# Memory queries computed already turned, and POOL's query weights placed behind its normalising, in a two-layer encoder trunk

## The chip, the cores and the metric

The kernel runs on one core of a Trainium2 chip. The metric is the device time of one execution in microseconds. The kernel before has a median of 1107.18 us over three runs (1106.81 to 1107.87).

## The reference

The model is a trunk of two layers on 512 tokens of width 1024 (batch 1), with 12 token heads (three key/value heads, four query heads to each), 4 memory heads, head dimension 64, and 256 memory tokens. Cut to what matters:

```python
for i in range(2):
    h = rms_norm(x, g_mix_pre[i])
    proj = h @ w_in[i]                       # q 768 | k 192 | v 192 | qm 256 columns
    tok = mixer_a(q, k, v, sink)             # layer 0: window of +-128, partial rotary, sink
          # or mixer_b(q, k, v)              # layer 1: all keys, q/k norms, 2-D rotary
    mkv = rms_norm(mem, mem_norm_g) @ w_mem_kv[i]
    mo = memory_attention(qm, km, vm)        # softmax(qm km^T / 8) vm, no rotary, no norm
    x = x + rms_norm(concat([tok, mo]) @ w_o[i], g_mix_post[i])
    h = rms_norm(x, g_ffn_pre[i])
    x = x + rms_norm((silu(h @ w_gate) * (h @ w_up)) @ w_down[i], g_ffn_post[i])
```

All is fp32. The memory queries qm get no rotary turn and no norm; apart from the row's RMS factor and the scale 1/8 they are a plain product.

## The kernel before

**Products.** Every fp32 operand is split into a high part rounded to fp32r and a remainder in fp32r (`split`, L283: the high part by ACT at L289 or POOL at L287, the remainder by DVE at L293 or POOL at L291; `split_scaled`, L300, the same with a factor per row or column). A product is three matmuls, high x high, high x low, low x high (`mm3`, L277, lines 279 to 281). In the attention the two parts of a query stand one above the other on the 128 partitions, 64 and 64, and the keys are held twice, as (high, low) in `ka` and as (low, high) in `kb`, so that two matmuls give all four terms of a score. Weights come through `unit` (L215): a DMA on SP's queue into a raw tile, and then a split into a pair of tiles, in two parts (NPART). `PACE` says for each unit which engine splits it: 0 is ACT and DVE, 1 gives the remainder to POOL, 3 gives both to POOL. In layer 0 that is 3 for the units of the query groups 2 and 3. Layer 1's units of those groups were split earlier, in layer 0's feed-forward part, and are only fetched as pairs.

**Order of the work.** PE's order is written out by hand. `mixer` (L684) puts every piece of a layer's mixer into one list with a position x, counted in heads: head hg is scored at x = hg, turned and applied to the values 1.7 heads later. The list is sorted and run through. The other engines issue in an order that a scheduler draws up from the program's order and its own estimate of times; each engine then runs strictly in that order, and waits on semaphores.

**Queries.** Queries are made in four groups of four heads, c = 0 to 2 for the token heads and c = 3 for the memory heads (`q_pieces`, L517). For each of four tiles of 128 tokens, eight k-steps of three matmuls each (128 tokens x 256 columns) go into a bank of PSUM. ACT takes it out with the row factor (L541: for c = 3 that is `rq`, minus the RMS factor over 8), then for c < 3 a rotary turn by DVE follows (L443 to L446 in layer 0, with POOL in layer 1). ACT and DVE split it (`parts`), PE transposes the four heads, high and low part together, into a second bank (`stage`, L559), and ACT copies that to `qT` (L560). Group c has its products at about x = 4c - 5, so group 3 begins at x = 7.1 (layer 0) or 6.97 (layer 1) and takes four heads' time, a tile to each head; the positions 12 and later belong to the memory heads.

**Memory heads.** `mem_pieces` (L385) makes keys and values of the memory; `keys` (L422) turns them on PE (L427, L432), with copies by ACT (L429) to `ka` and by DVE (L433) to `kb`. The second turned product uses the single bank tagged pv. `score_mem` (L601) scores two query tiles at a time (L613, L614). As the queries carry a negative factor, DVE takes a minimum per row (L615), which is the bias of ACT's exponent, whose scale is the constant -1 (L618). `normalise` (L624) divides by the sum on POOL (L634); `turn` (L637) transposes the probabilities (L644) and splits them (L289, L293); `value` (L651) applies them (L658, L659) and puts the head's two halves together by ACT (L666) and DVE (L667).

**Banks.** PSUM's eight banks go by tags: acc has two, s three in rotation, t two, pv one. The attention-out product (`heads_out`, L804) begins at x = 11.4 (11.3), before the memory heads, and takes acc, acc and s for its first three tiles.

**Start.** Layer 0's key/value products of the first two tiles (`kv_pieces`, L470, product lines L489 and L490) run in the order of the table `FIRST`: (tile, pair of k, kind), where HH is high x high, LH the low part of x, HL the low part of the weights. The parts of x are made by ACT (L306), POOL (L304) and DVE (L307).

Of the kernel before, what the change touches and what calls it, by code (L numbers as in the profile page):

```python
# [9 lines left out]
F32 = mybir.dt.float32  # L10
# [6 lines left out]
P = 128  # L17
S = 512
# [16 lines left out]
URGENT = 150  # L35
HH, HL, LH = range(3)
FIRST = ((0, 0, HH), (0, 1, HH), (0, 0, LH), (0, 1, LH), (0, 0, HL), (0, 1, HL), (1, 0, HH), (1, 1, HH), (1, 0, HL), (1, 1, HL),
         (0, 2, HH), (1, 2, HH), (0, 2, LH), (0, 3, HH), (1, 3, HH), (0, 3, LH), (1, 0, LH), (1, 1, LH), (1, 2, LH),
# [150 lines left out]
class Trunk:  # L189
    def __init__(self, tc, a):  # L190
        self.tc, self.nc, self.a, self.nraw, self.more, self.early = tc, tc.nc, a, 0, None, {}
        self.pairs, self.todo, self.stores = {}, [], []

# [20 lines left out]

    def unit(self, src, side=0, pool=None, parts=1, put=None, x=0, dst=None, key=None, g=None, raw=None, pair=None, early=None):  # L215

# [39 lines left out]
        box = []  # L256

        def first():
            box.append(load())
            dst[key] = box[0][1:]  # L260
            part(box[0], 0, n // NPART)

        put(x, first)
        for z in range(1, NPART):
            put(x + z / 4, lambda z=z: part(box[0], z * n // NPART, (z + 1) * n // NPART))

# [155 lines left out]
    def keys(self, k2, ka, kb, t, n):  # L422

        nc = self.nc
        tp = self.ps.tile([P, 4, P], F32, tag="t", name="tp", bufs=2)
        for h in range(n):
            nc.tensor.transpose(tp[:, h].bitcast(F32R), k2[:, h, :P], self.identr)  # L427
        c = slice(t * P, (t + 1) * P)
        nc.scalar.activation(ka[:, :, c], tp[:, :n], AF.Copy)  # L429
        tp = self.tagged("pv", "tp").rearrange("p (h n) -> p h n", n=P)  # L430
        for h in range(n):
            nc.tensor.transpose(tp[:, h].bitcast(F32R), k2[:, h, HD:], self.identr)  # L432
        nc.vector.tensor_copy(kb[:, :, c], tp[:, :n])  # L433

# [35 lines left out]
    def kv_pieces(self, l):  # L470
# [6 lines left out]
        def prod(t, st, u, which=None):  # L477
            self.ready(t)
            if u == 0 and which in (None, HH):
                st["ps"] = self.tagged("acc" if t < 2 else "s")  # L480
            ps = st["ps"]
            for k in (2 * u, 2 * u + 1):
# [3 lines left out]
                if which is None:  # L486
                    self.mm3(*args, k == 0, k == KD - 1)
                else:
                    nc.tensor.matmul(args[0], args[1 + (which == LH)], args[3 + (which == HL)],  # L489
                                     start=which == HH and k == 0, stop=which == HL and k == KD - 1)  # L490
            if u == 3 and which in (None, HL):
# [25 lines left out]
    def q_pieces(self, l, c, qTs, put, x0, lead):  # L517
        nc = self.nc
        w = {}
        for z in range(2):  # L520
            self.unit(self.a["wq"][l, c, z], self.side(l, "qw", 2 * c + z), put=put, x=x0 - lead + z * lead / 3, dst=w,
                      key=z, pair=("wq", l, c, z), early=("wq", z) if l == c == 0 else None)

        def prod(t, st, u):
# [10 lines left out]
            if u == 3:  # L535
                qx = self.core.tile([P, 4, HD], F32, tag="qx", name="qx", bufs=3)
                q = ps[:, :256].rearrange("p (h d) -> p h d", d=HD)
                if l == 1 and c < 3:
                    nc.scalar.activation(qx, q, AF.Copy, scale=self.rs[:, t:t + 1])
                else:  # L540
                    nc.scalar.activation(qx, q, AF.Copy, scale=self.rq[:, t:t + 1])  # L541
                st["qx"], st["r"] = qx, None
                if c < 3:
                    st["r"] = self.rope(l, qx, t, 4, 0)

# [7 lines left out]
        def stage(t, st):  # L553
            if c:
                tp = self.tagged("s" if c == 3 and t > 1 else "acc", "tp").rearrange("p (h n) -> p h n", n=P)
            else:
# [10 lines left out]
        return out  # L567


    def score(self, hd, i):  # L570
# [30 lines left out]
    def score_mem(self, hd, i):  # L601
# [9 lines left out]
        for z in range(2):  # L611
            qi = hd["q"]()[:, (i + z) * P:(i + z + 1) * P]
            nc.tensor.matmul(s[:, z], qi, hd["ka"](), start=True, stop=False)  # L613
            nc.tensor.matmul(s[:, z], qi, hd["kb"](), start=False, stop=True)  # L614
        nc.vector.tensor_reduce(nm[:, i:i + 2], s, axis=AX.X, op=OP.min)  # L615
        for z in range(2):
            p = self.core.tile([P, self.pbufs[0]], F32, tag="p", name="p", bufs=self.pbufs[1])
            nc.scalar.activation(p[:, :NMEM], s[:, z], AF.Exp, bias=nm[:, i + z:i + z + 1], scale=-1.0,  # L618
                                 accum_out=den[:, i + z:i + z + 1])
            hd["p"].append(p)  # L620
# [3 lines left out]
    def normalise(self, hd):  # L624
# [7 lines left out]
        for z, (k0, k1) in enumerate(hd["rng"]):  # L632
            n = (k1 - k0) * P
            self.pooled = nc.gpsimd.tensor_scalar(hd["p"][z][:, :n], hd["p"][z][:, :n], rd[:, z:z + 1], 1.0,  # L634
                                                  op0=OP.mult, op1=OP.mult)

# [47 lines left out]
    def mixer(self, l, mkp, late, tokp):  # L684
# [70 lines left out]
        self.mem_pieces(l, mk, put, xm, [pc["m0dur"], pc["m0dur"], pc["mdur"], pc["mdur"]], pc["mlag"], xw)  # L755
        for c in range(1, 4):
            x0 = 4 * c - 5 + pc["qoff"][c - 1]
            lay(self.q_pieces(l, c, qT, put, x0, pc["qlead"]), x0, pc["qstep"], pc["qlag"], lambda t, c=c: 4 * c + (t / 4 if c < 3 else t // 2 / 2 * pc["hstep"]))
        heads()
# [612 lines left out]
```

## Time and profile before

| | |
|---|---|
| profiled execution | 1108.23 us, of which the span of instructions is 1106.4 |
| median of three runs | 1107.18 us |
| granted TensorE clock | 0.998 |
| layer 0's mixer | from the start to about 166 us |
| layer 1's mixer | about 545 to 726 us |
| TensorE waited most for (all in the mixers) | DVE tl L293 2.6 us, DVE tok L667 2.4 us, DVE wlo L293 1.3 us |

The profile is of one execution, by the hardware's own recording. PE is TensorE's matmul, PEld its weight load, DVE VectorE, ACT ScalarE, POOL GpSimd, SP the queue of DMAs. A row of the timeline gives start, duration, engine, line of the kernel, operation, what it writes and reads, and in brackets how long the engine stood idle before and what ended that. Matmuls overlap: the time that one takes from the engine is the distance to the next one's start, not its duration.

### The profile page before, as it was taken

Reading aid. Unit: us, or ns where it says so; the run is one execution under the profiler, and the core shown is the slowest. Engines: PE = TensorE matmul, PEld = TensorE weight load, DVE = VectorE, ACT = ScalarE, POOL = GpSimd, SP = SyncE. Lnnn points to the kernel's source line nnn. Section 1 sums busy time; section 2 is a strip of 40 time slices with the busy share of each in tenths; the row PEclk is TensorE's granted clock in tenths of the full one; section 3 lists DMA queues with packets and bytes.
Section 4 is the critical chain, followed back from the end, with each engine's and each line's share of the span. In section 5 each row is a group of like instructions: output and inputs, shape, how many; then the busy total and the mean of one; then the engine's idle time right before and its main releaser. Section 6 shows DMA issues by size and latency. Waiting matters only on the chain.

```text
span 1106.4 us, 19515 instructions
## 1 busy us (share of the span) xinstructions
PE 1088.8 (98%) x7436; PEld 1000.2 (90%) x7436; DVE 842.2 (76%) x1433; ACT 659.3 (60%) x1357; POOL 194.9 (18%) x341
## 2 busy tenths in 40 slices
PE   9999999999999999999999999999999999999997
PEld 7899888999889989998898888879998899899986
DVE  7889876999458677875888988758995478668854
ACT  7679975865435535553567888747664365346531
POOL 5773231102000000000444542312000000000001
PEclk9999999999999999999999999999999999999999
DMA  9621017354832562335533221154236133422253
GB/s 335 248 78 39 20 35 252 116 165 133 303 124 86 180 221 78 113 101 190 195 124 115 77 77 39 39 189 154 72 106 207 55 100 115 129 76 97 83 165 115
DMA packets 40702, 142.44 MB, mean 129 GB/s; under 512 B 4768, under 2 KB 5152, under 8 KB 40480
## 3 DMA queue, kind: packets, MB, share of 16 engines
q1 hardware_dynamic: 40320, 140.80, 37.7%
q8 instruction: 58, 0.95, 0.4%
q10 hardware_dynamic: 288, 0.40, 0.1%
q14 instruction: 36, 0.29, 0.1%
HBM read 122.30 MB, written 18.87 MB: 128 GB/s over the span
## 4 chain that ended last, share of the span: by engine, by line
PE 84%; DVE 6%; ACT 4%; POOL 2%; DMA 2%; issue 1%; DVEq 0%; SPq 0%; POOLq 0%; ACTq 0%
PE ps L280 13%; PE ps L279 13%; PE ps L281 13%; PE ps L1043 12%; PE ps L1042 12%; PE ps L1041 12%; PE tp L644 3%; PE o L659 2%; PE o L658 2%; PE s L583 1%; PE s L584 1%; DVE mT L307 1%; ACT whi L289 1%; DVE tl L293 1%; DMA row<-in_x_dram 1%
## 5 line engine op out<-in xcount | busy, mean ns | idle before, releaser
L289 ACT ACTIVATE whi<-raw 128x1024 fp32r<-128x1024 f32 (+3 forms) x206 | 169.2, 839 | 175.9 <-PE ps L1043 73.5
L293 DVE TENSOR_TENSOR wlo<-raw,whi 128x1024 fp32r<-128x1024 f32 (+3 forms) x202 | 191.2, 961 | 74.5 <-ACT whi L289 71.3
L1042 PE MATMUL ps<-sf,wlo 128*128 128x256 f32 x640 | 179.7, 281 | 0.0
L1041 PE MATMUL ps<-sf,whi 128*128 128x256 f32 x640 | 179.7, 281 | 0.0
L1043 PE MATMUL ps<-sf,whi 128*128 128x256 f32 x640 | 179.7, 281 | 0.0
L280 PE MATMUL ps<-wlo,f 128*128 128x512 f32 (+1 forms) x360 | 138.6, 385 | 0.1
L279 PE MATMUL ps<-whi,f 128*128 128x512 f32 (+1 forms) x360 | 138.7, 385 | 0.0
L281 PE MATMUL ps<-whi,f 128*128 128x512 f32 (+1 forms) x360 | 138.4, 384 | 0.0
L1043 PE MATMUL ps<-a,whi 128*128 128x256 f32 x480 | 134.4, 280 | 0.0
L1041 PE MATMUL ps<-a,whi 128*128 128x256 f32 x480 | 134.3, 280 | 0.0
L1042 PE MATMUL ps<-a,wlo 128*128 128x256 f32 x480 | 133.8, 279 | 0.0
L1042 PEld LDWEIGHTS ps<-sf,wlo 128*128 128x128 f32 x640 | 121.4, 190 | 0.5
L1041 PEld LDWEIGHTS ps<-sf,whi 128*128 128x128 f32 x640 | 121.1, 189 | 0.5
L1043 PEld LDWEIGHTS ps<-sf,whi 128*128 128x128 f32 x640 | 121.4, 190 | 0.0
L322 POOL TENSOR_SCALAR e<-sso 128x1 f32<-128x1 f32 x8 | 3.4, 423 | 564.1 <-ACT junk L317 564.0
L634 POOL TENSOR_SCALAR p<-p,rd 128x256 f32<-128x256 f32 (+2 forms) x128 | 76.7, 618 | 101.4 <-DVE rd L631 46.2
L279 PE MATMUL ps<-whi,hT 128*128 128x256 f32 (+1 forms) x304 | 92.6, 305 | 0.0
L1042 PEld LDWEIGHTS ps<-a,wlo 128*128 128x128 f32 x480 | 90.5, 188 | 0.2
L1041 PEld LDWEIGHTS ps<-a,whi 128*128 128x128 f32 x480 | 90.4, 188 | 0.2
L1043 PEld LDWEIGHTS ps<-a,whi 128*128 128x128 f32 x480 | 90.1, 188 | 0.0
L280 PE MATMUL ps<-wlo,hT 128*128 128x256 f32 (+1 forms) x304 | 88.5, 291 | 1.3 <-DVE wlo L293 1.3
L281 PE MATMUL ps<-whi,hT 128*128 128x256 f32 (+1 forms) x304 | 88.2, 290 | 0.0
(207 smaller groups left out, 2703.9 us busy)
## 6 DMA issues: line engine op xcount, KB each, us to landing
raw<-in_wgu_dram SPq DMA_DIRECT2D x48, 512.0 KB, 4.5
raw<-in_wd_dram SPq DMA_DIRECT2D x44, 512.0 KB, 4.4
rb<-in_wgu_dram SPq DMA_DIRECT2D x40, 512.0 KB, 3.6
raw<-in_wo_dram SPq DMA_DIRECT2D x17, 512.0 KB, 4.1
raw<-in_wq_dram SPq DMA_DIRECT2D x16, 512.0 KB, 5.0
xt<-x SPq DMA_DIRECT2D x12, 512.0 KB, 5.2
raw<-in_wm_dram SPq DMA_DIRECT2D x8, 512.0 KB, 4.5
x<-y SPq DMA_DIRECT2D x8, 512.0 KB, 3.1
```

The lines of the kernel that those rows point to most:

```text
L279: mm(out, lh, rh, start=first, stop=False)
L280: mm(out, lh, rl, start=False, stop=False)
L281: mm(out, ll, rh, start=False, stop=last)
L289: a = nc.scalar.activation(hi, src, AF.Copy)
L293: b = nc.vector.tensor_sub(lo, src, hi.bitcast(F32))
L634: self.pooled = nc.gpsimd.tensor_scalar(hd["p"][z][:, :n], hd["p"][z][:, :n], rd[:, z:z + 1], 1.0, op0=OP.mult, op1=OP.mult)
L644: nc.tensor.transpose(tp[:, z], hd["p"][i][:, jj * P:(jj + 1) * P], self.ident)
L658: nc.tensor.matmul(o[:, c0:c1], hd["v"](j), th, start=(j == 0), stop=False, skip_group_check=True)
L659: nc.tensor.matmul(o[:, c0:c1], hd["v"](j), tl, start=False, stop=last, skip_group_check=True)
L1041: mm(out, wh[:, s], rh, start=start and k == 0, stop=False, skip_group_check=True)
L1042: mm(out, wl[:, s], rh, start=False, stop=False, skip_group_check=True)
L1043: mm(out, wh[:, s], rl, start=False, stop=k == 3, skip_group_check=True)
```

## The change

Five things are done at once.

1. The memory queries leave `q_pieces` and get a function of their own. The weights become the stationary operand, 128 columns (two heads) at a time, and 512 tokens stream past: two products z = 0, 1 of eight k-steps, each into an acc bank that holds two heads' queries with the head dimension on the partitions. No transposes follow. ACT copies head h of a bank to its own 64 partitions of `qT` as high part (`high`), DVE writes the remainder to the other 64 (`low`): for the odd heads the high part stands below, which the two forms of the keys allow. The eight k-steps of z = 0 take the two heads' time from x = 7.1, those of z = 1 the next two; the copies come at 0 and 0.5 (0 and 0.25) of a head after the end of the product, the remainders 0.2 (0.15) later.
2. These queries carry no factor. So `score_mem` takes a maximum, DVE multiplies it by `rq` (128x2), and the exponent's scale is a column of `rp` = -`rq`, made once per layer by POOL.
3. The copy of the memory keys to `kb` goes to ACT (token keys stay with DVE).
4. In layer 0 POOL's splits of query weights are issued behind the normalising of a certain head: group 2's units behind heads 0 and 1, group 3's behind heads 3 and 4.
5. In `FIRST`, tile 0's HH and LH of the first two pairs of k become H2: for each k, HH and then LH, where all HH ran first, then all LH.

```diff
-HH, HL, LH = range(3)
-FIRST = ((0, 0, HH), (0, 1, HH), (0, 0, LH), (0, 1, LH), (0, 0, HL), (0, 1, HL), (1, 0, HH), ...
+BEHIND = {(0, 2, 0): 0, (0, 2, 1): 1, (0, 3, 0): 3, (0, 3, 1): 4}
+HH, HL, LH, H2 = range(4)
+FIRST = ((0, 0, H2), (0, 1, H2), (0, 0, HL), (0, 1, HL), (1, 0, HH), ...
...
 def unit(...):
+        def behind(c0, c1):
+            with nullcontext() if after is None else self.tc.issue_after(self.pooled[after].ins):
+                part(box[0], c0, c1)
...
 def keys(...):
-        nc.vector.tensor_copy(kb[:, :, c], tp[:, :n])
+        if n == NMH:
+            nc.scalar.activation(kb[:, :, c], tp[:, :n], AF.Copy)
+        else:
+            nc.vector.tensor_copy(kb[:, :, c], tp[:, :n])
...
+    def memory_queries(self, l, qTs, put, x0, lead, step):
+        nc = self.nc
+        w, ps = {}, {}
+        for z in range(2):
+            self.unit(self.a["wq"][l, 3, z], self.side(l, "qw", 6 + z), put=put, x=x0 - lead + z * lead / 3, dst=w,
+                      key=z, pair=("wq", l, 3, z), after=BEHIND.get((l, 3, z)))
+        def prod(z, k):
+            if k == 0:
+                ps[z] = self.tagged("acc")
+            c = slice((k % 4) * 256 + P * z, (k % 4) * 256 + P * z + P)
+            wh, wl = [x[:, c] for x in w[k // 4]]
+            self.mm3(ps[z], wh, wl, self.hslice(0, k, 0, S), self.hslice(1, k, 0, S), k == 0, k == KD - 1)
+        rows = (slice(0, HD), slice(HD, P))
+        def high(z, h):
+            if z == h == 0:
+                qTs[3] = self.core.tile([P, 4, S], F32R, tag="qT", name="qT", bufs=2)
+                self.rp = self.small.tile([P, NT], F32, tag="rp", name="rp", bufs=2)
+                nc.gpsimd.tensor_scalar(self.rp, self.rq, -1.0, 1.0, op0=OP.mult, op1=OP.mult)
+            nc.scalar.activation(qTs[3][rows[h], 2 * z + h], ps[z][rows[h]], AF.Copy)
+        def low(z, h):
+            q = qTs[3][:, 2 * z + h]
+            nc.vector.tensor_sub(q[rows[1 - h]], ps[z][rows[h]], q[rows[h]].bitcast(F32))
+        for z in range(2):
+            for k in range(KD):
+                put(x0 + (2 * z + k / 4) * step, lambda z=z, k=k: prod(z, k))
+            for h in range(2):
+                x = x0 + 2 * (z + 1) * step + h * (0.25 if z else 0.5)
+                put(x, lambda z=z, h=h: high(z, h))
+                put(x + (0.15 if z else 0.2), lambda z=z, h=h: low(z, h))
...
 def score_mem(...):
-        nc.vector.tensor_reduce(nm[:, i:i + 2], s, axis=AX.X, op=OP.min)
+        mx = self.small.tile([P, 2], F32, tag="mx", name="mx", bufs=3)
+        nc.vector.tensor_reduce(mx, s, axis=AX.X, op=OP.max)
+        nc.vector.tensor_mul(nm[:, i:i + 2], mx, self.rq[:, i:i + 2])
...
-            nc.scalar.activation(p[:, :NMEM], s[:, z], AF.Exp, bias=nm[:, i + z:i + z + 1], scale=-1.0,
+            nc.scalar.activation(p[:, :NMEM], s[:, z], AF.Exp, bias=nm[:, i + z:i + z + 1],
+                                 scale=self.rp[:, i + z:i + z + 1],
                                  accum_out=den[:, i + z:i + z + 1])
...
 def mixer(...):
-        for c in range(1, 4):
+        for c in range(1, 3):
...
+        self.memory_queries(l, qT, put, 7 + pc["qoff"][2], pc["qlead"], pc["qstep"])
```

`issue_after` ties only the order on the named instruction's engine, here POOL.

More of the change, by code (lines that the diff above doesn't have):

```diff
@@ L213, in ahead, with unit @@
             self.stores = [(self.pairs[(name, *at)][z], pair[z].bitcast(F32)) for z in range(2)]
-    def unit(self, src, side=0, pool=None, parts=1, put=None, x=0, dst=None, key=None, g=None, raw=None, pair=None, early=None):
+    def unit(self, src, side=0, pool=None, parts=1, put=None, x=0, dst=None, key=None, g=None, raw=None, pair=None, early=None, after=None):
         nc, n = self.nc, src.shape[-1]
@@ L260, in first @@
             dst[key] = box[0][1:]
-            part(box[0], 0, n // NPART)
+            behind(0, n // NPART)
         put(x, first)
         for z in range(1, NPART):
-            put(x + z / 4, lambda z=z: part(box[0], z * n // NPART, (z + 1) * n // NPART))
+            put(x + z / 4, lambda z=z: behind(z * n // NPART, (z + 1) * n // NPART))
     def raw(self):
@@ L478, in prod @@
             self.ready(t)
-            if u == 0 and which in (None, HH):
+            if u == 0 and which in (None, HH, H2):
                 st["ps"] = self.tagged("acc" if t < 2 else "s")
@@ L488, in prod @@
                 else:
-                    nc.tensor.matmul(args[0], args[1 + (which == LH)], args[3 + (which == HL)],
-                                     start=which == HH and k == 0, stop=which == HL and k == KD - 1)
+                    for z in (HH, LH) if which == H2 else (which,):
+                        nc.tensor.matmul(args[0], args[1 + (z == LH)], args[3 + (z == HL)], start=z == HH and k == 0,
+                                         stop=z == HL and k == KD - 1)
             if u == 3 and which in (None, HL):
@@ L521, in q_pieces @@
             self.unit(self.a["wq"][l, c, z], self.side(l, "qw", 2 * c + z), put=put, x=x0 - lead + z * lead / 3, dst=w,
-                      key=z, pair=("wq", l, c, z), early=("wq", z) if l == c == 0 else None)
+                      key=z, pair=("wq", l, c, z), early=("wq", z) if l == c == 0 else None, after=BEHIND.get((l, c, z)))
         def prod(t, st, u):
@@ L537, in prod @@
                 q = ps[:, :256].rearrange("p (h d) -> p h d", d=HD)
-                if l == 1 and c < 3:
+                if l:
                     nc.scalar.activation(qx, q, AF.Copy, scale=self.rs[:, t:t + 1])
@@ L554, in stage @@
             if c:
-                tp = self.tagged("s" if c == 3 and t > 1 else "acc", "tp").rearrange("p (h n) -> p h n", n=P)
+                tp = self.tagged("acc", "tp").rearrange("p (h n) -> p h n", n=P)
             else:
@@ L755, in mixer @@
         self.mem_pieces(l, mk, put, xm, [pc["m0dur"], pc["m0dur"], pc["mdur"], pc["mdur"]], pc["mlag"], xw)
-        for c in range(1, 4):
+        for c in range(1, 3):
             x0 = 4 * c - 5 + pc["qoff"][c - 1]
-            lay(self.q_pieces(l, c, qT, put, x0, pc["qlead"]), x0, pc["qstep"], pc["qlag"], lambda t, c=c: 4 * c + (t / 4 if c < 3 else t // 2 / 2 * pc["hstep"]))
+            lay(self.q_pieces(l, c, qT, put, x0, pc["qlead"]), x0, pc["qstep"], pc["qlag"], lambda t, c=c: 4 * c + t / 4)
+        self.memory_queries(l, qT, put, 7 + pc["qoff"][2], pc["qlead"], pc["qstep"])
         heads()
```

12 lines of the change are left out of this document (5 added, 7 removed).

## The prediction

> **What bounds the kernel now.** I read the page first, then the idle time of TensorE (the view of waits), then busy times by stretch, then the timeline of the stretches that the change touches.
>
> ```profile
> PE 1088.8 (98%) x7436; PEld 1000.2 (90%) x7436; DVE 842.2 (76%) x1433; ACT 659.3 (60%) x1357; POOL 194.9 (18%) x341
> PE 84%; DVE 6%; ACT 4%; POOL 2%; DMA 2%; issue 1%; DVEq 0%; SPq 0%; POOLq 0%; ACTq 0%
> ```
>
> TensorE is busy 98% of the span and holds 84% of the chain that ended last. So a matmul that is no longer issued is worth its slot, unless another engine ends last where it stood. The stretches with busy times (us: length, PE, PEld, DVE, ACT, POOL) show two such places beside this change:
>
> ```profile
> 120.00:138.00 18.00, 16.58 (x122) 15.29 (x121) 16.77 (x47) 17.73 (x52) 4.62 (x9) 1.00 0.10 30
> 680.00:690.00 10.00, 9.35 (x57) 7.78 (x56) 9.23 (x17) 9.95 (x24) 2.70 (x4) 1.00 0.19 76
> ```
>
> In the last part of layer 0's token heads ACT is busy 17.73 of 18 us and PE 16.58; in layer 1's, ACT 9.95 of 10 and PE 9.35. There a saved matmul can turn into idle time.
>
> **The transposes that go.** The turned product gives queries with head dimensions on the partitions, so the memory queries' 16 transposes per layer (four groups of four, L559) are removed. PE's timeline around one group:
>
> ```profile
> 676.32 0.60 PE L644 MATMUL tp<-cst,p 128*128 128x128 f32 x4
> 676.67 0.54 PE L559 MATMUL tp<-identr,q 128*128 128x128 f32 x4
> 677.05 0.35 PE L279 MATMUL ps<-whi,hT 128*128 128x256 f32 x1
> ```
>
> The group holds PE from 676.67 to the next start at 677.05: 0.38 us (its 0.54 us overlaps the next). Two layers times four groups: 8 x 0.38 = 3.0 us.
>
> **The products.** Per layer 4 tiles x 8 k x 3 = 96 matmuls of 256 columns become 2 x 8 x 3 = 48 of 512. Starts three matmuls apart:
>
> ```profile
> 679.21 0.28 PE L279 MATMUL ps<-whi,hT 128*128 128x256 f32 x1
> ...
> 679.57 0.28 PE L279 MATMUL ps<-whi,hT 128*128 128x256 f32 x1
> ...
> 689.36 0.40 PE L279 MATMUL ps<-whi,th 128*128 128x512 f32 x1
> ...
> 690.06 0.39 PE L583 MATMUL s<-ka,qT 128*128 128x512 f32 x1
> ```
> ```profile
> 399.82 0.39 PE L279 MATMUL ps<-whi,f 128*128 128x512 f32 x1
> ...
> 400.50 0.39 PE L279 MATMUL ps<-whi,f 128*128 128x512 f32 x1
> ```
>
> 256 columns take 0.36/3 = 0.120 us, 512 columns 0.70/3 = 0.233 here in the mixer and 0.68/3 = 0.227 in the down product. 96 x 0.120 = 11.5 against 48 x 0.233 = 11.2 or 48 x 0.227 = 10.9: 0.3 to 0.6 us per layer. The rows are rounded, so I take near the low end, 0.35, and 0.7 us for both. PE's work falls by 3.7 us.
>
> **ACT and DVE.** Median durations (min/median/max ns) of what goes and of the nearest rows to what comes:
>
> ```profile
> L541 ACT ACTIVATE qx<-ps,rq x20: 453/466/502, 28.9 to 682.5; 128x256 f32<-128x256 f32 x20
> L289 ACT ACTIVATE q<-qx x32: 400/417/438, 33.6 to 687.1; 128x256 fp32r<-128x256 f32 x32
> L560 ACT ACTIVATE qT<-tp x32: 575/598/629, 48.5 to 695.2; 128x512 fp32r<-128x512 f32 x32
> L666 ACT ACTIVATE tmp<-o x32: 589/594/597, 71.5 to 724.6; 64x512 f32<-64x512 f32 x32
> L618 ACT ACTIVATE p<-s,nm x32: 462/472/506, 136.5 to 716.9; 128x256 f32<-128x256 f32 x32
> L293 DVE TENSOR_TENSOR q<-qx,q x32: 407/426/805, 41.4 to 687.6; 128x256 fp32r<-128x256 f32 x32
> L667 DVE TENSOR_TENSOR tok<-o,tmp x32: 672/688/697, 72.1 to 725.2; 64x512 f32<-64x512 f32 x32
> L631 DVE RECIPROCAL rd<-den x32: 160/174/180, 61.7 to 717.5; 128x4 f32<-128x4 f32 x32
> ```
>
> Per layer ACT loses 4 x (0.47 + 0.42 + 0.60) = 5.9 us and gains four copies of 64x512 (4 x 0.59 = 2.4, by L666; half the partitions cost what the whole does) and two key copies of 128x512 (0.6 each, by L560). DVE loses four q remainders (1.7) and the two key copies, and gains four remainders of 64x512 (4 x 0.69 = 2.8, by L667) and eight products of 128x2 (at most 8 x 0.17 = 1.4, by the reciprocal).
>
> In 120 to 138 ACT loses about half of the 5.9 us and gains the second half's two copies, so near 2 us net; DVE there trades two q remainders for two larger ones, about even. DVE's 16.77 us then ends last where ACT's 17.73 did: the stretch may shrink by some 0.7 us while PE would shrink by about 1.2 (two to three groups and half the products' gain). I put 0.5 us as given back (bounds: 0.8 gained, 1.2 given back). In layer 1 the idle time is one wait:
>
> ```profile
> 686.36 0.30 PE L644 MATMUL tp<-cst,p 128*128 128x128 f32 x1 [0.65 <-DVE tl L293]
> ```
>
> It hangs on ACT's queue, not on PE; PE comes some 1.5 us earlier (three groups and the products), ACT about half a us to none. I put 0.5 us given back (bounds: 0.4 gained, 1.0 given back).
>
> The exponent now takes its scale from a column of 128x1 instead of a constant. L541 has such a scale and costs 0.466 for 256 columns where L289, without, costs 0.417, so 0 to 0.1 us each, 16 per layer; with the product behind the maximum, the chain score, maximum, exponent grows by 0.2 to 0.3 us. The memory heads' stretch has room on all three but for the end, where TensorE waits for the previous head's output:
>
> ```profile
> 722.83 0.47 PE L658 MATMUL o<-th,vm 128*128 128x512 f32 x1 [0.68 <-DVE tok L667]
> ```
>
> That wait is DVE's queue; I put +0.25 us for both layers (0 to 1.0). The Trainium skill (ScalarE: Activation LUTs, section What ACT_TABLE_LOAD costs) says each 128x1 pointer operand adds about 93 ns to an ACTIVATE. Those rows lie between none and that; by the page ACT gets back 32 x 0.093 = 3.0 us of its relief, an estimate, and the sum stays, since this stands where ACT has room.
>
> **The memory keys' copy.** The second turned product of a key tile (L432) uses the one bank tagged pv, so the next tile's must wait until the first is copied out. That copy moves from DVE to ACT, behind ACT's queue. Layer 1, PE, ACT, and PE again where the first head is turned; then layer 0:
>
> ```profile
> 598.92 0.50 PE L432 MATMUL tp<-identr,k 128*128 128x128 f32 x4
> ```
> ```profile
> 599.15 0.60 ACT L429 ACTIVATE kma<-tp 128x512 fp32r<-128x512 f32 x1
> 599.63 0.71 ACT L595 ACTIVATE p<-s,nm 128x512 f32<-128x512 f32 x1
> ```
> ```profile
> 603.21 0.38 PE L644 MATMUL tp<-cst,p 128*128 128x128 f32 x2
> 603.80 0.33 PE L644 MATMUL tp<-cst,p 128*128 128x128 f32 x1 [0.22 <-POOL p L634]
> ```
> ```profile
> 60.30 0.50 PE L432 MATMUL tp<-identr,k 128*128 128x128 f32 x4 [0.77 <-DVE kmb L433]
> ```
>
> In layer 1 the second tile's product starts at 598.92 unhindered. ACT starts the first tile's other copy only at 599.15; the moved copy can follow at 599.7 and ends near 600.4: PE, and all behind it in order, waits 1.5 us. About 0.9 us of it comes back at 603, where PE idles for head 0's probabilities in two steps (the last of three matmuls that should need 0.1 us each starts 0.6 late, and another wait follows). Net +0.55 (0 to 1.5). In layer 0 the wait of 0.77 for DVE becomes one for ACT: +0.15 (-0.8 to +0.3).
>
> **POOL and the first products.** POOL's timeline in layer 0:
>
> ```profile
> 74.28 1.30 POOL L291 TENSOR_TENSOR wlo<-raw,whi 128x512 fp32r<-128x512 f32 x1
> 75.56 2.25 POOL L634 TENSOR_SCALAR p<-p,rd 128x256 f32<-128x256 f32 x4
> ...
> 88.34 2.10 POOL L634 TENSOR_SCALAR p<-p,rd 128x256 f32<-128x256 f32 x4 [4.52 <-ACT th L289]
> ```
>
> Head 2's normalising stood behind weight splits; the memory weights now come behind heads 3 and 4, where POOL idles 4.52 us before head 4: room for one unit's two remainders (1.30 each) and its two roundings. The weights are needed only at 7.1 heads by the program's order, two heads on. I put -0.3 (-0.6 to +0.6).
>
> At the start, xh wh and xl wh now alternate:
>
> ```profile
> 6.61 2.40 PE L489 MATMUL ps<-whi,hT 128*128 128x384 f32 x8 [0.20 <-ACT whi L289]
> ...
> 9.54 1.10 PE L489 MATMUL ps<-whi,hT 128*128 128x384 f32 x4
> ```
> ```profile
> 8.98 1.54 POOL L304 TENSOR_SCALAR hT<-xT,gcol 128x128 fp32r<-128x128 f32 x4
> ```
>
> The eight take 2.40 us; back to back they would take about 1.6 (seven starts 0.174 apart, an estimate midway between the slots of 256 and 512 columns, and a last one of at most 0.4): 0.8 us of gaps while ACT makes the next weights, which the xl products can fill; so the 9.54 group could start 0.5 us earlier. But that group needs tile 1's odd columns from POOL, whose run from 8.98 ends at 10.52: it stays. I take 0 (0.5 gained at best).
>
> **Sum.** -3.7 + 0.5 + 0.5 + 0.25 + 0.55 + 0.15 - 0.3 + 0 = -2.05 us. The profiled execution took 1108.23 us for a span of 1106.4, 1.05 above the median 1107.18, so its sum would be 1106.2; put on the median, 1105.1 us.
>
> **Rivals.** *All of the removed work lands*: the waits at the keys and in the two ACT-bound stretches don't come, because ACT's lighter queue runs ahead of where the rows show it. For: 5.9 us per layer off ACT where it is fullest. Against: DVE is nearly as full. -3.7 - 0.3 = -4.0: 1103.2 us.
>
> *POOL's splits hold up DVE.* A DVE product of 128x64 took 1.29 us while POOL split weights, 0.29 while it did not:
>
> ```profile
> 55.25 1.29 DVE L443 TENSOR_TENSOR rt<-qx,cst 128x64 f32<-128x64 f32 x1
> ...
> 60.48 0.29 DVE L443 TENSOR_TENSOR rt<-qx,cst 128x64 f32<-128x64 f32 x1
> ```
> ```profile
> 53.91 2.56 POOL L291 TENSOR_TENSOR wlo<-raw,whi 128x512 fp32r<-128x512 f32 x2
> ```
>
> The splits move on behind heads 0, 1, 3 and 4, the last two near 84 to 95 us, beside the rotary products; some 1.5 us of DVE delay there reach PE: 1106.6 us. The Trainium skill (SBUF — State Buffer, section Who interferes with whom) has the rule: DVE with two SBUF inputs and a reading GpSimd exclude each other for a whole instruction. The trace agrees in this place (1.29 against 0.29).
>
> *The second bank comes free late: slower.* Each half of the queries keeps one acc bank until its last remainder is off; the attention-out product's second tile (L279, 689.36 above) needs the second half's bank. Today the last tile leaves its bank early and its remainder follows late:
>
> ```profile
> 682.47 0.50 ACT L541 ACTIVATE qx<-ps,rq 128x256 f32<-128x256 f32 x1
> ...
> 687.57 0.61 DVE L293 TENSOR_TENSOR q<-qx,q 128x256 fp32r<-128x256 f32 x1 [0.16 <-ACT q L289]
> ```
>
> If that lag of 5.1 us stays, the last remainder, placed a quarter of a head later (heads 2 and 4 on POOL are 12.8 us apart, so 1.6 us) and behind another of 0.69, runs from 689.9 to 690.5, while PE wants the bank at 689.36 - 1.5 = 687.9: a wait of 2.6 us per layer. -2.05 + 5.3 = +3.2: 1110.4 us. It decides from a lag of about 2.5 us on. Against: two steps instead of four, straight from the bank, and ACT relieved.
>
> **Chances.** The forecast 0.50 (1104.0 to 1106.6 us), all lands 0.26, POOL 0.12, the bank 0.12. A measurement of this kernel tells about 0.2%, 2.2 us, from no change, so faster means below 1105.0: the second case and two fifths of the first, 0.46; slower 0.12; the same 0.42. The range runs from 1102.4, a little below the full gain, to 1108.0, where the bank's case begins: 0.18 left out.
>
> **What would show it.** No L559 in the last quarter of the token heads, 48 products of 128x512 at 0.23; L432's wait on ACT near 600; DVE instead of ACT as the fullest engine in 120 to 138; first group at 9 us, then a longer wait for POOL; the attention-out product's waits. It is wrong if the mixers' idle time on PE changes by over 3 us, whatever the sum.

## The result and the profile after

The changed kernel takes 1113.82 us (median of 4 runs, 1113.30 to 1114.34) where the kernel before, run beside it, takes 1106.99 (1106.72 to 1107.87, 4 runs): a ratio of 1.0057 [1.0045, 1.0069], so 6.8 us slower. The prediction was 1105.1 with a range up to 1108.0. The profiled execution of the changed kernel took 1113.55 us for a span of 1111.8. That of the kernel before took 1108.23, 1.2 us above the median 1106.99, so differences read from the two profiles add up to about 5.4 us and not to 6.8.

The page's busy line of the changed kernel (engine, busy us, share of the span, instructions):

```profile
PE 1092.6 (98%) x7308; PEld 997.3 (90%) x7308; DVE 843.8 (76%) x1445; ACT 660.3 (59%) x1345; POOL 198.3 (18%) x343
```

TensorE has 128 matmuls less than before (7436) and is busy 3.8 us longer (1088.8 before), where the prediction took 3.7 us off. Some matmuls became slower. Stage by stage, from the starts of TensorE's matmuls in both traces (us):

| stage | before | after |
|---|---|---|
| layer 0, first matmul to the first turn of the attention-out result | 187.99 | 187.02 |
| layer 0's feed-forward, from the third such turn to layer 1's first key product | 340.09 | 340.58 |
| layer 1's mixer, from the third group of transposes in it (549.14 us before) to the first feed-forward matmul | 209.52 | 210.45 |
| layer 1's feed-forward | 340.67 | 345.75 |

The first row runs past the 166 us given above for layer 0's mixer because it takes in the rest of the attention-out product. The pieces between the rows (13.5 and 6.4 us) differ by less than 0.1 us. The two mixers together change by 0.0 us, and layer 1's feed-forward, of which the diff touches no line, takes 5.1 us more. Busy times in the same 60 us of that feed-forward (length, then PE, PEld, DVE, ACT, POOL with instructions, granted clock, DMA share, GB/s), before and after:

```profile
985.00:1045.00 60.00, 60.00 (x517) 60.00 (x516) 53.23 (x78) 35.75 (x60) 0.00 (x0) 1.00 0.30 98
```
```profile
985.00:1045.00 60.00, 60.00 (x502) 60.00 (x501) 50.64 (x75) 35.18 (x59) 0.00 (x0) 1.00 0.33 103
```

TensorE never idles in either, the granted clock is 1.00 in both, and 517 matmuls of 256 columns have become 502. The longest unbroken run of them, 636, takes 74.20 us before and 76.31 after: 116.7 and 120.0 ns each. Its first matmul and the first of the product behind it, before and after:

```profile
977.15 0.28 PE L1041 MATMUL ps<-a,whi 128*128 128x256 f32 x1
...
1051.35 0.39 PE L279 MATMUL ps<-whi,f 128*128 128x512 f32 x1
```
```profile
980.47 0.28 PE L1088 MATMUL ps<-a,whi 128*128 128x256 f32 x1
...
1056.78 0.39 PE L284 MATMUL ps<-whi,f 128*128 128x512 f32 x1
```

The 512-column matmuls of the down product keep 227 ns.

### The profile page after: what moved, and what is told of

Same layout as the page of the kernel before. It is cut to its first block, busy times and chain, and to the rows that moved or that the text cites. A ratio compares the mean times of both kernels' runs of the same rounds, so it can differ in the third digit from the quotient of the medians.

```text
span 1111.8 us, 19277 instructions
## 1 busy us (share of the span) xinstructions
PE 1092.6 (98%) x7308; PEld 997.3 (90%) x7308; DVE 843.8 (76%) x1445; ACT 660.3 (59%) x1345; POOL 198.3 (18%) x343
## 4 chain that ended last, share of the span: by engine, by line
PE 86%; DVE 6%; ACT 4%; POOL 1%; issue 1%; DMA 1%; DVEq 0%; SPq 0%; POOLq 0%; ACTq 0%
PE ps L284 13%; PE ps L285 13%; PE ps L286 13%; PE ps L1090 12%; PE ps L1089 12%; PE ps L1088 12%; PE tp L690 3%; PE o L705 2%; PE o L704 2%; DVE tl L298 1%; PE s L626 1%; PE s L627 1%; DVE tok L713 1%; DMA row<-in_x_dram 1%; PE tp L566 0%
## 5 line engine op out<-in xcount | busy, mean ns | idle before, releaser
L286 PEld LDWEIGHTS ps<-whi,f 128*128 128x128 f32 x360 | 67.6, 188 | 13.6
L285 PEld LDWEIGHTS ps<-wlo,f 128*128 128x128 f32 x360 | 67.7, 188 | 12.9
L284 PEld LDWEIGHTS ps<-whi,f 128*128 128x128 f32 x360 | 67.7, 188 | 12.8
```

The costliest lines, as they stand in the source:

```text
L284: mm(out, lh, rh, start=first, stop=False)
L285: mm(out, lh, rl, start=False, stop=False)
L286: mm(out, ll, rh, start=False, stop=last)
```

## The experiments

Two theories stood against each other. *Addresses*: the change makes two new small tiles (2 x 32 and 3 x 32 bytes in each partition) in the pool `small`, the second from the bottom of the memory; by the compiled program's layout this puts everything above it up by 160 bytes, the weights' pairs `whl` from byte 24000 to 24160, while the pools counted from the top, with layer 1's activations, stay. For layer 1's 256-column matmuls the start of the moving operand (the activations) minus that of the stationary one (the weights) goes from 32 to 128, modulo 256 bytes; from here on this is called the difference. *Streams*: the changed instruction streams reach into the feed-forward in some other way. Kernels of one batch are compared with runs of the kernel before on the same chip (1107.3 to 1107.7).

### Unused bytes in the kernel before

One line in `run`, a tile that nothing reads or writes; the instructions stay:

```diff
             self.mhalf = glob.tile([P, 4], F32, name="mhalf")
+            glob.tile([P, 40], F32, name="pad")
```

> Theory 1 (placement): the change's two new small tiles (rp and mx) push every tile of the left half of SBUF, the weights among them, up by 160 bytes, while layer 1's feed-forward activations, in the right half, stay; a 256-column product is slower where its stationary and its moving operand begin at the same address modulo 64. The kernel before with 160 unused bytes and nothing else then loses what the changed kernel lost in the feed-forward layers: layer 1's triples of matmuls go from 0.350 to 0.360 us, its feed-forward from 340.7 to about 345.8 us, the total from 1107.0 to about 1112.5. Theory 2 (rival): the slower products of layer 1 come from the instruction streams (128 matmuls fewer shift PE's program, other orders on ACT and DVE), not from addresses: then no difference, 1107.0.

1114.64 us, ratio 1.0062 [1.0047, 1.0077]; layer 1's feed-forward 345.97, the mixers 187.37 and 209.66. Its window is the changed kernel's:

```profile
985.00:1045.00 60.00, 60.00 (x502) 60.00 (x501) 50.58 (x75) 34.82 (x59) 0.00 (x0) 1.00 0.31 106
```

160 unused bytes cost the kernel before all that the change cost. The streams theory falls. To find the law, the same line with 8 and 16 elements (32 and 64 bytes), and with 8 in the changed kernel (192 bytes in all):

> Theory 1 with the period 64: a shift of 32 bytes gives the same remainder as 160, so the same loss, about 1112.5 us. If the period were 256 or more, 32 and 160 should differ. Theory 2: 1107.0.

> Theory 1 with the period 64: a shift of 64 bytes changes nothing, 1107.0 us. If any shift at all hurts (or the period is 128 or more), it loses as well, towards 1112.5. Theory 2: 1107.0.

> The changed kernel with 32 unused bytes, so that the shift is 192, a multiple of 64. Theory 1: layer 1's feed-forward is back at 340.7 us, the first layer's about 0.5 shorter, the total about 1108.0 us, and what is left against 1107.0 is the mixers'. Theory 2: still 1113.8.

1115.11 (1.0067 [1.0050, 1.0084]), 1110.66 (1.0030 [1.0018, 1.0042]) and 1115.04 (1.0068 [1.0053, 1.0083]); layer 1's feed-forward 346.41, 343.43 and 346.45. A period of 64 bytes is refuted: neither 64 nor 192 restores the pitch (the time from one matmul's start to the next one's). By the compiled programs' layouts the difference is 128 with 160 bytes, and 0, 224 and 96 in these three.

### The change at the old addresses, and two of the mixers' terms

```diff
-                self.rp = self.small.tile([P, NT], F32, tag="rp", name="rp", bufs=2)
+                self.rp = self.core.tile([P, NT], F32, tag="rp", name="rp", bufs=2)
...
-        mx = self.small.tile([P, 2], F32, tag="mx", name="mx", bufs=3)
+        mx = self.core.tile([P, 2], F32, tag="mx", name="mx", bufs=3)
```

> The change with its two new small tiles (2 x 32 and 3 x 32 bytes) taken from the mixers' own pool, which lies above the weights, so that every tile of the feed-forwards lies where it lay before. The instructions of every engine are the change's. Theory 1 (the slower feed-forward is a matter of addresses): feed-forward of layer 1 back from 345.75 to 340.7 us, of layer 0 at 340.1, mixers as in the change (187.0 and 210.3), 1107.0 to 1108.5 in all, where the kernel before has 1107.2 to 1107.7. Theory 2 (something else that the change does, reaching into the feed-forward): it stays at 345.7 and 1113.8.

1107.65 us (11 runs) against 1107.29 (21): 1.0003 [0.9994, 1.0012]. The feed-forwards are back at 340.09 and 340.33. With its tiles out of the way the change is worth nothing that can be measured; the 6.8 us were the addresses.

On top of it, layer 1's second key copy back on DVE (`self.more` is set in layer 1 alone):

```diff
-        if n == NMH:
+        if n == NMH and self.more is None:
```

> The same, and in layer 1 the second copy of the memory keys goes back to VectorE (in layer 0 it stays on ScalarE). If the wait of 1.44 us at 598.6 is this copy alone, as the prediction had it, that wait goes and layer 1's mixer comes down from 210.3 by the net price that the prediction put on it, 0.55 (0 to 1.5), to 209.7; 1106.5 to 1108 in all. If the wait came from the bank rather than from the copying engine, nothing changes.

1106.86 us (11 runs; 0.9997 [0.9988, 1.0006]). The second key product of layer 1, changed kernel and this one:

```profile
600.16 0.51 PE L437 MATMUL tp<-identr,k 128*128 128x128 f32 x4 [1.30 <-ACT kmb L439]
```
```profile
597.18 0.46 PE L432 MATMUL tp<-identr,k 128*128 128x128 f32 x4
597.47 0.50 PE L437 MATMUL tp<-identr,k 128*128 128x128 f32 x4
```

The wait is this copy: without it L437 follows 0.29 us behind L432.

Instead of that, the memory scores without the row's factor:

```diff
-        mx = self.core.tile([P, 2], F32, tag="mx", name="mx", bufs=3)
-        nc.vector.tensor_reduce(mx, s, axis=AX.X, op=OP.max)
-        nc.vector.tensor_mul(nm[:, i:i + 2], mx, self.rq[:, i:i + 2])
+        nc.vector.tensor_reduce(nm[:, i:i + 2], s, axis=AX.X, op=OP.min)
...
-                                 scale=self.rp[:, i + z:i + z + 1],
+                                 scale=-1.0,
```

> The same as the run with its small tiles moved, but the memory heads' scores are not scaled by row: the maximum is taken as in the kernel before, without the product behind it, and the exponent has a constant scale. (The scores stay unscaled, so this part of the computation is left out.) If the longer chain score, maximum, exponent is what layer 1's mixer loses between 685 and 710 (0.5 to 1.4 us against the saved groups), its mixer falls from 210.3 by about 1 us, to 209.3, and layer 0's by 0.3 to 0.5. If the loss is the waits for the second bank and the copied halves, the mixers stay at 187.0 and 210.3 within 0.3.

1106.86 us (one run; this kernel leaves out the row's factor, so it computes other probabilities). Layer 1 loses 0.04 us from memory head 0 to memory head 2, where the changed kernels lose 0.96 (table below). The exponent's groups, changed kernel and this one (busy us, mean ns):

```profile
L663 ACT ACTIVATE p<-s,nm,rp 128x256 f32<-128x256 f32 x32 | 17.7, 559 | 4.5 <-DVE nm L660 3.3 <-PE tp L690 0.9
```
```profile
L661 ACT ACTIVATE p<-s,nm 128x256 f32<-128x256 f32 x32 | 14.8, 470 | 5.8 <-DVE nm L658 5.0 <-POOL p L678 0.6
```

The column costs 89 ns. That lies just under the prediction's upper bound of 0.1 us. The Trainium skill (ScalarE: Activation LUTs, section What ACT_TABLE_LOAD costs) has about 93 ns for such an operand, and the trace agrees with it.

### Two more terms: POOL's order and the second bank

Both on the kernel with the keys mended.

```diff
-BEHIND = {(0, 2, 0): 0, (0, 2, 1): 1, (0, 3, 0): 3, (0, 3, 1): 4}
+BEHIND = {}
```

> The run with mended addresses and layer 1's second key copy on VectorE, and in it POOL's query weights no longer held behind its normalising (the table is empty, nothing else). From head 5 to head 7 of layer 0 the changed kernels lose 0.85 us against the kernel before, beside POOL's splits at 80 to 93 us. If that is the price of the new order on POOL (the second rival: splits that hold up others), head 7 comes 0.85 us earlier against head 5 than with the table; if the order on POOL is a gain of 0.3 (the prediction), the heads 2 to 5 come later by 0.3 and nothing else moves. In all between 1106.0 and 1107.2, where the run with the table had 1106.86.

```diff
+        def soon(f, z, h):
+            with self.urgent() if z else nullcontext():
+                f(z, h)
...
-                put(x, lambda z=z, h=h: high(z, h))
-                put(x + (0.15 if z else 0.2), lambda z=z, h=h: low(z, h))
+                put(x, lambda z=z, h=h: soon(high, z, h))
+                put(x + (0.15 if z else 0.2), lambda z=z, h=h: soon(low, z, h))
```

> The run with mended addresses and layer 1's second key copy on VectorE, and in it the two copies and two remainders of the second half of the memory queries come ahead in ScalarE's and VectorE's order, so that the second bank comes free early. Third rival (the second bank comes free late): the wait of 1.60 us near 131 us in layer 0 goes, or falls under 0.3. Whether that shortens the mixer is open: if TensorE is what counts there, layer 0's mixer falls by 1 to 1.6 us; if ScalarE and VectorE end last in that stretch (the prediction's reason for what is given back), the wait comes back in the memory heads and the mixer stays within 0.4.

1107.51 us (1.0003 [0.9994, 1.0012]) and 1106.56 (0.9992 [0.9983, 1.0001]). Lengths between landmarks (the first score of a head, `last` the last score of head 11, `m` the memory heads), as the mean of four kernels with the mixers of before (it and its three padded ones) and what the others differ from that, us. "Change" is the mean of four kernels with the change's mixers; apart from the rows marked *, where they lie up to 0.4 from it, the four of either kind lie within 0.08 of their mean. "The end" is the first turn of the attention-out result in layer 0 and the first feed-forward matmul in layer 1. The last four columns are one profile each.

| stretch | before | change | keys | keys, no table | keys, bank | no scale |
|---|---|---|---|---|---|---|
| layer 0, head 0 to 1 | 6.31 | -0.91 | -0.91 | +0.13 | -0.92 | -0.90 |
| head 5 to 7 | 13.41 | +0.84 | +0.84 | 0.00 | +0.82 | +0.86 |
| head 9 to 11 | 13.56 | -0.74 | -0.72 | -0.73 | -0.74 | -0.72 |
| head 11 to last | 6.06 | +1.19 | +1.19 | +1.19 | -0.20 | +1.17 |
| last to m3 | 17.55 | -1.50 | -1.51 | -1.50 | -0.70 | -1.30 |
| m3 to the end | 37.97 | +0.37 | +0.36 | +0.38 | +0.97 | -0.03 |
| **head 0 to the end** | 134.75 | -0.90 | -0.85 | -0.59 | -0.91 | -1.10 |
| layer 1, head 1 to 3 | 15.44 | +0.59 | +0.01 | -0.04 | -0.01 | +0.59 |
| head 8 to 11 | 25.36 | -0.76 | -0.76 | -0.81 | -0.78 | -0.75 |
| head 11 to last | 6.78 | +0.38 | +0.38 | +0.37 | -0.18 | +0.38 |
| m0 to m2 * | 13.35 | +0.96 | +0.75 | +1.22 | +1.21 | +0.04 |
| m2 to the end * | 52.51 | +0.06 | -0.08 | -0.09 | -0.09 | +0.34 |
| **head 0 to the end *** | 166.08 | +1.15 | +0.24 | +0.61 | +0.06 | +0.56 |

POOL's table gains 1.04 us at head 0 to 1 and loses 0.84 at heads 5 to 7. The gain isn't the normalising, which in layer 0 comes only at 60 us: it is VectorE. Without the table POOL splits the third group's weights beside VectorE's rotary product, and TensorE later waits at a second key product; with it (the kernel with the keys mended) POOL is idle there, the product is short and the wait is gone:

```profile
53.63 2.54 POOL L296 TENSOR_TENSOR wlo<-raw,whi 128x512 fp32r<-128x512 f32 x2
54.99 1.26 DVE L451 TENSOR_TENSOR rt<-qx,cst 128x64 f32<-128x64 f32 x1
60.17 0.51 PE L437 MATMUL tp<-identr,k 128*128 128x128 f32 x4 [0.90 <-ACT kmb L439]
```
```profile
54.72 0.23 DVE L451 TENSOR_TENSOR rt<-qx,cst 128x64 f32<-128x64 f32 x1
58.87 0.51 PE L437 MATMUL tp<-identr,k 128*128 128x128 f32 x4
```

Behind the long product VectorE's first masked scores (L632) come 1.0 us later, counted from head 0's start, and ScalarE's exponents and key copies behind them. At heads 5 to 7 the memory queries' weights are split instead, and there VectorE's remainder of a token query takes 0.89 us beside a split where it takes 0.42 without. POOL there, changed kernel and the one without the table:

```profile
87.74 2.10 POOL L680 TENSOR_SCALAR p<-p,rd 128x256 f32<-128x256 f32 x4 [1.11 <-ACT th L294]
89.81 1.36 POOL L292 TENSOR_SCALAR whi<-raw 128x512 fp32r<-128x512 f32 x2
91.15 2.53 POOL L296 TENSOR_TENSOR wlo<-raw,whi 128x512 fp32r<-128x512 f32 x2
```
```profile
88.24 2.10 POOL L680 TENSOR_SCALAR p<-p,rd 128x256 f32<-128x256 f32 x4 [4.53 <-ACT th L294]
95.04 2.05 POOL L680 TENSOR_SCALAR p<-p,rd 128x256 f32<-128x256 f32 x4 [4.70 <-DVE rt L451]
```

The attention-out product's second tile near 132 us: before, with the keys mended, and with the bank freed early:

```profile
132.83 0.48 PE L279 MATMUL ps<-whi,th 128*128 128x512 f32 x1
```
```profile
132.54 0.50 PE L284 MATMUL ps<-whi,th 128*128 128x512 f32 x1 [1.60 <-DVE qT L603]
```
```profile
131.32 0.48 PE L284 MATMUL ps<-whi,th 128*128 128x512 f32 x1
```

The wait of 1.60 us is for a remainder of the second half (L603) and goes when these come early. But of the 1.39 us won there only 0.06 is left at layer 0's end (of 0.56 in layer 1, 0.18): the memory heads wait by as much more.

### The law of the addresses

A kernel of nothing but the feed-forward's kind of matmuls, 8 triples for each of 16 x 16 pairs of start addresses, 32 bytes apart:

```python
for a in range(0, 128, 8):
    for b in range(0, 128, 8):
        seven(ps[(b // 8) % 2], a, b)
```

> The disputed cost by itself. Nothing but the feed-forward's kind of matmul triple (weights high x data high, weights low x data high, weights high x data low; 128 columns of weights, 256 columns of data, fp32r), 8 triples for each pair of starting addresses: weights at 0 to 480 bytes above a first address in steps of 32, data likewise, 16 x 16 pairs; then, with ScalarE and VectorE copying and subtracting 128x1024 all the while, 16 weight addresses against two data addresses. It computes none of the reference. If TensorE alone is sensitive to where weights and data lie, the pitch of the first part varies between 0.1167 and 0.120 us over the pairs, by a law of the difference (32 modulo 512 the fastest, 0 the slowest). If the sensitivity comes from the other engines' traffic (theory of contention), the first part is flat, near 0.1167 or below, and only the second part varies. If it hangs on something else in the kernel (the code's place, the program's length), both parts are flat.

With nothing else at work the pitch varies with the difference, data (the moving operand) minus weights modulo 256 bytes (mean ns over 32 pairs each, lowest and highest behind it):

| 0 | 32 | 64 | 96 | 128 | 160 | 192 | 224 |
|---|---|---|---|---|---|---|---|
| 119.5 | 118.3 | 117.9 | 119.4 | 118.9 | 117.7 | 115.0 | 117.8 |
| 119.3-120.0 | 117.6-118.3 | 117.7-118.0 | 119.3-120.0 | 118.4-119.1 | 117.1-118.8 | 114.1-117.9 | 117.6-118.5 |

Two pairs in TensorE's timeline, 21 matmuls from the first row to the second, a difference of 0 and one of 192:

```profile
214.69 0.28 PE L47 MATMUL ps<-mh,wl 128*128 128x256 f32 x1
...
217.20 0.28 PE L47 MATMUL ps<-mh,wl 128*128 128x256 f32 x1
```
```profile
231.76 0.28 PE L47 MATMUL ps<-mh,wl 128*128 128x256 f32 x1
...
234.16 0.28 PE L47 MATMUL ps<-mh,wl 128*128 128x256 f32 x1
```

2.51/21 = 119.5 ns and 2.40/21 = 114.3 ns. In the second part, begun beside ScalarE and VectorE, 32 gave 116.7 to 117.0 and 192 gave 113.6 or 117.6 to 117.8. Neither 32 as the fastest nor a period of 512, the law that was expected, came. But the sensitivity is there without the other engines; their traffic falls as its cause.

The ranges have a pattern that points at what ran just before. Call the 16 data starts with one weight start a row. From a row's eighth data start on, all 18 pairs with one difference agree within 0.1 ns (192: 114.1 to 114.2). The other values stand among a row's first seven pairs, right after the data start has jumped back by 480 bytes.

Does the kernel follow? First by the grid's best value (192) for all 256-column matmuls of both feed-forwards, on the kernel with the keys mended:

```diff
+            glob.tile([P, 24], F32, name="pad")
...
+            self.hp.tile([P, 48], F32, tag="gap", name="gap", bufs=1)
...
+            self.hp.tile([P, 16], F32, tag="gap2", name="gap2", bufs=1)
```

> The run with mended addresses and layer 1's second key copy on VectorE, with three unused tiles more: 96 bytes ahead of the weights, 192 bytes between the weights and the first layer's turned activations, 64 behind these. By the run of matmuls alone the pitch of 256 columns goes by the difference of the two start addresses modulo 256: 0 gave 119.5 ns, 32 gave 118.3, 128 gave 118.9, 192 gave 114.2. All 256-column matmuls of both feed-forwards now have 192, and the 512-column ones of the down product keep 0. If that law holds beside the other engines: feed-forward of layer 1 from 340.4 to 336 us, of layer 0 from 340.1 to 332, the whole to 1095. If it is the law of the idle chip only, and the kernel's own five points (32 the fastest) are another law: both stay within 2 us or get slower by up to 5, 1105 to 1115.

1104.53 us, 0.9972 [0.9960, 0.9984], in two groups of three (1102.8 to 1103.2 and 1105.8 to 1106.3). In the profiled execution, one of the longer three, layer 0's feed-forward takes 338.55, layer 1's 342.26: 117.8 ns, not 114.2. The grid's law held in kind, not in size. Then the changed kernel with 96 unused bytes at the other end, so that the difference is again that of before (32 modulo 256):

```diff
+            self.pool(top, "edge", side="right").tile([P, 24], F32, name="edge")
```

> The change as it is, small tiles and all, with one unused tile of 96 bytes at the other end of the memory: the tiles that are counted from that end (the matmuls' data in layer 1's feed-forward, and a part of it in layer 0's) move down by 96 where the weights had moved up by 160, 256 in all against each other. If the difference of the two start addresses modulo 256 is what counts: feed-forward of layer 1 back from 345.75 to 340.7 us, of layer 0 at 340.1 to 340.6, 1107.5 to 1108.5 in all. If the addresses themselves count (the weights', still 160 higher), layer 1's feed-forward stays at 345 to 346 and the whole at 1113.8.

1107.98 us, 1.0004 [0.9995, 1.0013]; layer 1's feed-forward 340.43:

```profile
985.00:1045.00 60.00, 60.00 (x516) 60.00 (x515) 53.20 (x79) 35.76 (x60) 0.00 (x0) 1.00 0.31 97
```

The weights still lie 160 bytes higher than before, so for this pair of starts it is the difference that counts, modulo 256, and not the address.

### A combination

On the kernel with the keys mended and the bank freed early:

```diff
+BEHIND = {(0, 2, 0): 0, (0, 2, 1): 1}
...
+            self.hp.tile([P, 8], F32, tag="gap", name="gap", bufs=1)
...
+            self.hp.tile([P, 56], F32, tag="gap2", name="gap2", bufs=1)
```

> What the runs favour, put together: small tiles in the mixers' pool; layer 1's second key copy on VectorE; the memory queries' second half copied out ahead of the queue; on POOL only the weights of the third query group behind the normalising (its head 0 to 1 gained 0.9 us, the memory queries' weights lost 0.85 at heads 5 to 7); and 32 unused bytes between the weights and layer 0's turned activations, 224 behind them, so that the half of layer 0's feed-forward matmuls that had a difference of 0 modulo 256 (119.6 ns) gets 32 (116.7 ns in layer 1). If the difference modulo 256 counts in the kernel too: feed-forward of layer 0 from 340.1 to 337.5 us, of layer 1 340.3, layer 0's mixer 185.5 to 186.5, layer 1's 209.4, in all 1103 to 1104.5, below both kernels. If the address counts by itself, layer 0's feed-forward stays at 340 and the whole is 1106.

1106.24 us, 0.9986 [0.9977, 0.9995]. Layer 0's feed-forward fell to 336.20, more than the 337.5 expected, but its mixer took 192.04. The feed-forward's surplus is in the other half of its matmuls, whose difference was 32 all along: in the kernel before they took 118.2 ns in blocks of twelve between blocks with a difference of 0, and here, between blocks with 32, 116.7 ns. With the short table head 2's normalising stands behind the memory queries' weights (POOL):

```profile
76.37 1.19 POOL L292 TENSOR_SCALAR whi<-raw 128x512 fp32r<-128x512 f32 x2
77.53 1.43 POOL L296 TENSOR_TENSOR wlo<-raw,whi 128x512 fp32r<-128x512 f32 x1
78.95 2.05 POOL L684 TENSOR_SCALAR p<-p,rd 128x256 f32<-128x256 f32 x4
```

Heads 1 to 5 took 5.2 us more. TensorE waits only 1.23 and 1.34 us there (ending at 77.0 and 79.5 us); the rest goes with its clock, which the profile shows granted at 0.50 from 79.1 us on, for 6.8 us. Five microseconds of that stretch, here and in the next kernel:

```profile
80.00:85.00 5.00, 4.95 (x23) 4.96 (x24) 2.81 (x11) 3.22 (x10) 2.64 (x4) 0.50 0.31 93
```
```profile
80.00:85.00 5.00, 4.84 (x39) 4.54 (x38) 4.70 (x15) 3.69 (x11) 4.29 (x7) 1.00 0.00 0
```

In no other kernel's trace does the clock fall before the last matmul, and in none does TensorE idle for more than 1.8 us within 4 us, once the first 10 us are over; that the two waits made the clock fall is likely, but was not tested by itself. The eleven executions fit: the seven with a mean clock of 0.996 or 0.997 took 1106.1 to 1107.5 us, the four with 0.998 or 0.999 took 1104.5 to 1105.8. The entries that lost 0.84 at heads 5 to 7 are also what keeps head 2 free. With the full table again:

> The combination with the change's own full table of what stands behind POOL's normalising. In the combination with the half table layer 0's mixer took 192.04 us, 5.3 more than with the full one, lost between heads 2 and 4, where POOL's rows show head 2's normalising behind ten splits of the memory queries' weights (72.70 to 78.95 us). If that is the cause, layer 0's mixer is back at 186.3 to 187.2, the feed-forward of layer 0 stays at 336.2, and the whole is 1102 to 1103, faster than both kernels. If the moved activations are what slows layer 0's mixer, it stays near 192 and the whole at 1106.

1103.21 us (1102.80 to 1103.54), 0.9962 [0.9948, 0.9975]: faster than the kernel before by 4.3 us. Layer 0's feed-forward, the kernel before and this one:

```profile
420.00:485.00 65.00, 65.00 (x549) 65.00 (x548) 54.43 (x82) 38.59 (x66) 0.00 (x0) 1.00 0.33 103
```
```profile
420.00:485.00 65.00, 65.00 (x560) 65.00 (x559) 55.41 (x82) 38.90 (x66) 0.00 (x0) 1.00 0.31 99
```

549 matmuls become 560. The mixer takes 187.75 us, above the expected 187.2: the attention-out product, 512 columns wide, went from 226.7 to 233.3 ns over its unbroken run of 114 with its new difference (224 for 0), 0.75 us.

## Why the prediction was wrong

**The step that failed** is the sum itself. It took the profiled time of before and added only what happens where the diff stands, so all other code was costed at nothing. The new tiles' 160 bytes moved the weights against layer 1's activations, and some 1900 matmuls there, 256 columns wide, took 2.7 ns more each on average: 5.1 us, with 0.5 more in layer 0. Shown from both sides, by unused bytes in the kernel before and by moved tiles in the changed one. The test that the prediction named (TensorE's idle time in the mixers, over 3 us) pointed at the wrong place: in the profiles it rose by only 1.9 us, from 8.4 to 10.4, and the loss is no idle time and not in the mixers. Of the 8.7 us between forecast and result this term is 5.6 and the mixers' miss, below, 2.3.

**The mixers** by themselves were also forecast too well: from head 0 on they change by -0.90 and +1.15, so +0.25 for -2.05.

- *Layer 1's key copy*: right. Net +0.59 for +0.55; the wait is 1.30 us for 1.5.
- *Layer 0's key copy*: right, +0.13 for +0.15, seen once POOL's table is away: the wait of 0.77 for DVE becomes one of 0.90 for ACT. With the table there is no such wait at all.
- *POOL*: the net was right (-0.85 against -0.59 without the table, so -0.26 for -0.3), its making was not. The prediction looked for the gain in head 2's normalising; the gain of 1.04 and the loss of 0.84 at heads 5 to 7 both show the second rival's mechanism, POOL's splits holding up DVE, taken away in one place and put into another, the loss at about half that rival's 1.5. (Its row of 0.29 us at 60.48 still began beside a split, which ended at 60.69; without any the same product takes 0.23.)
- *The third rival's wait* came, at 1.6 us of its 2.6 in layer 0 and 0.33 in layer 1, but is not its price: freeing the bank gave back 0.06 and 0.18 us.
- *The longer chain* score, maximum, exponent was the term most mis-sized: 0.20 and 0.59 us against the mean of the change's kernels (0.21 and 0.87 against the one it was cut from), for 0.25 in all.
- *Removed groups and products less what is given back*: forecast -1.22 per layer behind head 7 or 8, the chain's half included; measured -0.72 in layer 0 and +0.65 in layer 1. Each group's 0.38 us shows (-0.74 and -0.76 for two), and is given back between head 11 and the end. The signs it named came (in 120 to 138 us DVE is now the fullest at 17.07, ACT has 16.72), but not the relief. Of layer 1's miss of 1.9, the chain beyond what was put down for it (0.5 to 0.7) and the bank (0.18) explain 0.6 to 0.9; the rest lies where ACT and DVE are full, and stays open.
- *First products*: right as far as the traces show, though not tried by itself. The next group starts at 8.96 us instead of 9.54, and then waits for POOL:

```profile
8.96 0.33 PE L498 MATMUL ps<-whi,hT 128*128 128x384 f32 x1
9.94 0.82 PE L498 MATMUL ps<-whi,hT 128*128 128x384 f32 x3 [0.64 <-POOL hT L309]
```

The last of the `FIRST` products starts at 15.9 to 16.1 us in four kernels that start like the one before and at 15.7 to 16.1 in those that start like the change.

## What to carry to other kernels

A cost estimate made edit by edit holds only if the edit leaves the addresses of everything else alone: compare the memory layouts of both programs before trusting the sum, and put small new tiles where nothing long-lived lies above them. Where a kernel is bound by long unbroken runs of matmuls, a few unused bytes between weights and data are worth trying, with the pitch of such a run as the measure. A saved matmul in a stretch whose other engines are full comes back as a wait a little later, and so does a removed wait: measure from landmark to landmark up to the end of the stretch.

## What the runs showed of the hardware

The pitch of back-to-back fp32r matmuls depends on the start address of the moving operand minus that of the stationary one, modulo 256 bytes, at a full granted clock and without any idle time. For 256 columns in the kernel, over the run of 636 in layer 1 (the activations move): 116.7 ns at 32, 117.8 at 192, 118.3 at 224, 120.0 at 0, 96 and 128. For 512 columns (the attention-out product of layer 1, an unbroken run of 114, the weights move) the best is another: 226.8 at 0, 229.1 at 64, 232.3 at 128, 233.3 at 224 and 233.4 at 32. The Trainium skill (SBUF — State Buffer, section Who interferes with whom) has TensorE's read ports for moving data and for weights as independent and knows contention only on the port pair that VectorE and GpSimd share; the bare grid, with no other engine at work, differs from that by up to 5 ns of 119.5, and the measurement decides.

One difference can have two paces (114 or 117.8 ns at 192, 116.7 or 118.2 at 32). What ran just before has a part in it: matmuls with 32 went from 118.2 to 116.7 ns when only their neighbours' difference changed. That does not explain 117.8 ns at 192 throughout a run of 636; why was not found.
